# A trunk of two layers on one core: the last token tile's last chunk in two halves, norms of fewer single-column operations, stores on two queues

## The chip, the core and the metric

The kernel runs on one core of a Trainium2 chip. A core has a tensor engine (PE, with its weight loads shown as PEld), a vector engine (DVE), a scalar engine (ACT), GpSimd (POOL) and a sync engine (SP) that here only issues transfers; 16 DMA engines move data between the chip's memory and the core. Each engine works through its own instructions in order, and they wait for one another by semaphores. The metric is device time in microseconds, the median of several executions.

## The reference, cut to what matters

256 tokens of 2048 features pass two layers. Layer 0 mixes with a long convolution and a short gated one, layer 1 with centred moving means; after each comes a squared-ReLU MLP with 8192 hidden features. Every part has a norm before and behind it:

```python
def rmsnorm(u, g):
    r = lax.rsqrt(jnp.mean(u * u, axis=-1, keepdims=True) + NORM_EPS)
    return u * r * g

for i in range(2):
    h = rmsnorm(x, g[0])
    m = mixer of layer i (h)
    x = x + rmsnorm(m, g[1])
    h = rmsnorm(x, g[2])
    f = square(relu(h @ mlp_w1[i])) @ mlp_w2[i]
    x = x + rmsnorm(f, g[3])
return x
```

## The kernel before

The tokens are two tiles of 128 (t = 0 and 1). Where tokens lie on the partitions, `xt` [128, 2, 2048] holds x and `ac` [128, 2, 2048] the sum of a projection, in four chunks of 512 features. All weights stream from memory once, in pieces of [128, 1024], by SP's queue into four buffers (`raw`). For precision each operand of a matmul is split into a high and a low part: for weights ACT copies the high part (`whi`, L131) and DVE subtracts it for the low part (`wlo`, L145), and each product is made of three matmuls, high by high, high by low, low by high. The order of work on every engine is written out by hand: instructions are issued in the order in which the Python code runs, and each engine keeps that order.

The MLP's second projection runs in four groups g of 2048 hidden features and four chunks n of 512 columns. A chunk has 8 pieces, and `a_piece` (L251) makes the six matmuls of 512 columns of one piece and one token tile (L258, L259, L260), so a chunk is 48 matmuls a tile. `after_2` (L813) adds the result, scaled by a number for each token, to `ac` (L819), and for the last group `sums` (L667) squares it on ACT with a running sum into a column of `st` (L668), and DVE multiplies the gain of the norm in (L822). `st` is a small tile of single columns.

`rsqrt_of` (L338) makes one over the root mean square of a tile's tokens: a sum over the four parts (L342), a root on ACT (L343), the mean on DVE (L344), then what a `filler` brings, then a reciprocal (L347) and one step of refinement (L348, L349, L350), each on one column. `m_rms` uses it for `ac`, `x_rms` for x; `residual` (L690) then adds a chunk of `ac` times that column to `xt`.

Between two phases stands `boundary` (L745): the last chunk of a phase and the first of the next run token tile by token tile, so that the matmuls of one tile cover the norm, the residuals and the transposes (`x_to_features`, L698) of the other. `unit_pass` (L714) runs one tile over the pieces and issues such steps at given pieces. Layer 1 has two such changeovers: from layer 0's MLP to the pooling (around 1110 to 1145 us), where `m_rms` of tile 1 and `x_rms` of tile 0 stand close together, and from the pooling to the MLP (1155 to 1185 us), where `m_rms` of tile 0 has the gain of the last pooling group as its filler (L931) and PE has nothing to do until `xt` is there. `turn_first` (L799) turns the MLP's first hidden features.

The end is written in three lines: the last chunk for tile 0, then `finish(0)`, the last chunk for tile 1, then `finish(1)`. `finish` (L984) calls `m_rms`, and for each of four chunks `residual` and a store of [128, 512] on SP's queue (L988).

Of the kernel before, what the change touches and what calls it, by code (L numbers as in the profile page):

```python
# [29 lines left out]
# Column tiles of the input projection: x0 0-7, x1 8-15, v 16-23, gb 24-31, gc 32-39, xv 40-47.  # L30
# [13 lines left out]
# Column tiles after which the convolution's parts are issued. For each quarter of the channels and each half:  # L44
# the filter's last layer, and from the quarter's first column tile on, u to tokens, forward and inverse transform.
# [4 lines left out]
# The column tile after which 1 / rms is made.  # L50
R_AT = 2

# Offsets of the per-channel parameters in their array.
# [5 lines left out]
class Stream:  # L59
    """Pieces of [128, 1024] in the order of their use: loaded ahead, split ahead, then used."""  # L60
# [28 lines left out]
    def raw(self, ap, fn, place=None):  # L89
        """fn gets the piece in its turn; place() gives a tile for it that isn't one of the ring's."""  # L90
        self.items.append(("r", ap, (fn, place)))
# [22 lines left out]
    def hi(self, upto):  # L114
        """The high part of the next piece, if a slot is free."""
        if self.n_split >= self.n_dma:
            return False
        i = self.n_split
        kind, ap, what = self.items[i]
        if kind == "w":  # L120
            if what > upto:
                return False
            pool, tag, bufs = self.rings[self.ring_at % len(self.rings)]
            old = self.history[tag]
            if len(old) >= bufs and old[-bufs] >= self.released:
                return False
            old.append(what)
            self.ring_at += 1
            hi = pool.tile([P, 1024], F32R, tag=tag + "h", name="whi", bufs=bufs)
            lo = pool.tile([P, 1024], F32R, tag=tag + "l", name="wlo", bufs=bufs)  # L130
            self.nc.scalar.copy(hi, self.raws[i])  # L131
            self.half.append((i, what, hi, lo))
        elif kind == "r":
            what[0](self.own.pop(i) if what[1] else self.raws.pop(i))
        elif kind == "s":
            what()
        self.n_split += 1
        return True

    def lo(self):  # L140
        """The low part of the oldest piece that has only its high part."""
        if not self.half:
            return False
        i, what, hi, lo = self.half.pop(0)
        self.nc.vector.tensor_tensor(lo, self.raws.pop(i), hi.bitcast(F32), ALU.subtract)  # L145
        self.parts[what] = (hi, lo)
        return True
# [8 lines left out]
    def pump(self, at):  # L156
        """Issue what may run ahead of piece `at`."""
        while True:
            moved = self.load()
            if not self.held or at not in self.parts:  # L160
                upto = at if self.held else at + self.ahead
                moved = self.hi(upto) or moved
                while self.half and (not self.held or self.half[0][1] <= at):
                    moved = self.lo()
            if not moved:
                return
# [13 lines left out]
def trunk(ctx: ExitStack, tc: tile.TileContext, x, xT_d, win_d, wout_d, w1s_d, w1_d, w2_d, pw_d,  # L180
# [23 lines left out]
    st = common.tile([P, 48], F32, name="st")  # L204
    A.dma_start(out=par, in_=par_d)
    make_identity(nc, ident)
    V.memset(eps, EPS)
    A.copy(st[:, 46:47], eps)

    # ---- the stream of pieces  # L210
# [8 lines left out]
    def split_to(hi, lo, src, scale=None):  # L219
        """hi + lo = src * scale, each of 12 bits."""  # L220
        if scale is None:
            A.copy(hi, src)  # L222
            V.tensor_tensor(lo, src, hi.bitcast(F32), ALU.subtract)  # L223
        else:
            A.activation(hi, src, AF.Copy, scale=scale)
            V.scalar_tensor_tensor(lo, src, scale, hi.bitcast(F32), ALU.mult, ALU.subtract)
# [5 lines left out]
    # ---- matmuls  # L232
    def b_tile(pieces, width):
        """[128 features, tokens] of one tile of 128 features."""
# [16 lines left out]
    def a_piece(acc, t, src, k0, part, first, last):  # L251
        """Adds two k-tiles of 512 features to acc [128 tokens of tile t, 512]."""
        hi, lo = part
        for kk in range(2):
            sh = src(k0 + kk)[:, t * P:(t + 1) * P]
            sl = src(k0 + kk)[:, 256 + t * P:256 + (t + 1) * P]
            a, b = hi[:, kk * 512:(kk + 1) * 512], lo[:, kk * 512:(kk + 1) * 512]
            mm(acc, sh, a, start=first and kk == 0, stop=False)  # L258
            mm(acc, sh, b, start=False, stop=False)  # L259
            mm(acc, sl, a, start=False, stop=last and kk == 1)  # L260
# [11 lines left out]
    # ---- mixer of layer 0  # L272
# [44 lines left out]
    def add_squares(q):  # L317
        """The sum of x * x over the k-tiles of a piece, added to that of the pieces before."""
# [18 lines left out]
    # st: 0-7 sums of squares by part; 8.. work by tile  # L337
    def rsqrt_of(parts, t, filler=()):  # L338
        """st[:, 8 + 4 t] = 1 / sqrt(mean + eps)."""
        w = st[:, 16 + 8 * t:24 + 8 * t]  # L340
        r = st[:, 8 + 4 * t:9 + 4 * t]
        V.tensor_reduce(w[:, 0:1], parts, axis=AX.X, op=ALU.add)  # L342
        A.activation(w[:, 1:2], w[:, 0:1], AF.Sqrt, bias=eps, scale=1.0 / D)  # L343
        V.tensor_scalar(w[:, 2:3], w[:, 0:1], 1.0 / D, EPS, ALU.mult, ALU.add)  # L344
        for f in filler:
            f()
        V.reciprocal(w[:, 3:4], w[:, 1:2])  # L347
        V.scalar_tensor_tensor(w[:, 4:5], w[:, 3:4], w[:, 3:4], w[:, 2:3], ALU.mult, ALU.mult)  # L348
        V.tensor_scalar(w[:, 5:6], w[:, 4:5], -0.5, 1.5, ALU.mult, ALU.add)  # L349
        V.tensor_tensor(r, w[:, 3:4], w[:, 5:6], ALU.mult)  # L350
        return r

# [62 lines left out]
    # -- pieces of the filter  # L415
    def filter_layer(acc, bias, dst):
        """dst = sin(freq * (acc + bias))"""
# [25 lines left out]
    def filter_3(q, l):  # L443
        """Sum and difference of the two filters for 256 channels, split."""
# [18 lines left out]
    def filter_4(q):  # L463
        """The filters' transform: cosine part, sine part, cosine part, by the even and the odd frequencies."""
# [19 lines left out]
    # -- the convolution  # L484
    us, Us, Pq, x0s = {}, {}, {}, {}

    def to_tokens(c):
        """u of 128 channels, as its even and odd halves about the middle, to [tokens, channels], split."""
# [53 lines left out]
    # -- what follows each tile of the input projection  # L542
# [57 lines left out]
    def spread_r():  # L600
        """1 / rms of each token, on every partition."""
# [53 lines left out]
    def spread(row, n):  # L655
        """512 columns of a row, on every partition."""
# [17 lines left out]
    def m_rms(t, *filler):  # L674
        return rsqrt_of(st[:, 4 * t:4 * t + 4], t, steps(*filler))
# [4 lines left out]
    def inv_square(t):  # L680
        """st[:, 40 + t] = 1 / (mean + eps)"""
# [6 lines left out]
    def residual(t, n):  # L688
        """x += ac / rms"""
# [24 lines left out]
    def unit_pass(units, t, src, post, slots, release):  # L714
        """The products of one token tile with the pieces of a chunk; slots: what to issue before a unit."""
# [17 lines left out]
    def steps(*fs):  # L733
        """Closures of (function, arguments...)."""
        return [lambda f=f: f[0](*f[1:]) for f in fs]
# [9 lines left out]
    def boundary(units, src, post, uslots, switch, units2, src2, post2, vslots, wslots):  # L745
        """The last chunk of a phase and the first of the next: tile 1 of the one runs while tile 0's norms and
        transposes are made, tile 0 of the other while tile 1's are."""
# [10 lines left out]
    # ---- output projection of layer 0  # L758
# [8 lines left out]
    ysrc = lambda k: YT[:, k]  # noqa: E731  # L767
    xsrc = lambda k: xT[:, k]  # noqa: E731
# [4 lines left out]
    class Mlp:  # L773
# [52 lines left out]
        def run(self):  # L826
            """All but the first chunk and the last, which is returned with its source."""
            for g in range(4):
# [16 lines left out]
                fsrc = lambda k, fts=fts: fts[k // 4][:, k % 4]  # noqa: E731  # L845
# [17 lines left out]
    class Later:  # L863
        """Stands for what `switch` makes."""
# [25 lines left out]
    # ---- layer 1: pooling  # L890
# [24 lines left out]
    def pool_sums(t, g):  # L915
        """The moving sums less the counts' share: [128 tokens, 512] of tile t."""
# [67 lines left out]
    def finish(t):  # L984
        m_rms(t)
        for n in range(4):
            residual(t, n)
            nc.sync.dma_start(out=out[t][:, ch(n)], in_=xt[:, t, ch(n)])  # L988

    unit_pass(units, 0, fsrc, m1.post_last, {"end": steps((finish, 0))}, False)  # L990
    unit_pass(units, 1, fsrc, m1.post_last, {"end": steps((finish, 1))}, True)
# [4 lines left out]
def _constants():  # L996
# [5 lines left out]
    # The even positions, then the odd ones.  # L1002
# [4 lines left out]
    # [quarter][lag][tile of lags][the same 256 channels twice]  # L1007
# [8 lines left out]
    def table(first, second):  # L1016
        """Two [256, 256] tables, [tile of rows][first hi, lo, second hi, lo][256] for each row of a tile."""
# [3 lines left out]
    # The frequencies (2 f + 1) / 1024 of a turn: the even f, then 255 less each of them.  # L1021
    n = np.arange(256, dtype=np.float64)
    f = (2.0 * np.concatenate([n[0::2], 255.0 - n[0::2]]) + 1.0) * math.pi / 512.0
    # [lag / 2][even or odd lag][cosine, sine][hi, lo][even f]
# [6 lines left out]
    # [token < 128][even or odd f][plus or minus][hi, lo][f]  # L1031
# [17 lines left out]
def _arrange(x, norm_g, mix_w_in, hy_short_w, hy_short_b, hy_filt_w1, hy_filt_b1, hy_filt_w2, hy_filt_b2,  # L1049
# [3 lines left out]
    chan = lambda v: v.reshape(-1, P).T  # noqa: E731  # L1053

    def features(w):
        """[D, n] -> tiles of 128 columns: [tile][row in k-tile][k-tile, column]"""
        return c(w.reshape(KT, P, -1, P).transpose(2, 1, 0, 3)).reshape(-1, P, KT * P)

    def tokens(w, kt):
        """[kt * 128, n] -> chunks of 512 columns: [chunk][row in k-tile][k-tile, column]"""  # L1060
# [48 lines left out]
```

## Time and profile before

| | us |
|---|---|
| runs | 1895.4, 1896.15, 1896.45 (median 1896.15) |
| profiled execution, from its first to its last instruction (span) | 1894.5 |
| PE busy | 1866.0 (98%) |
| DVE busy | 1212.3 (64%) |
| ACT busy | 860.5 (45%) |
| last matmul starts | 1884.72 |
| first and last residual of tile 1 start | 1888.71, 1890.70 |

The profiled execution has no time of its own beside its span; what the runs' clock takes in around the span shows in the runs alone. Matmuls are pipelined: a row's length is longer than the step from one matmul to the next, so steps are read from starts. A row of the timeline gives the start, the length, the engine, the line of the program, the operation, the tiles written and read, the shape, and in brackets how long the engine had been idle and what ended that.

### The profile page before, as it was taken

To read this page: it belongs to the slowest core of one execution; us is meant where nothing else is said; L and a number is where in the kernel's file an instruction comes from. 1 tells how busy PE (TensorE), PEld (TensorE's weight loads), DVE (VectorE), ACT (ScalarE), POOL (GpSimd) and SP (SyncE) were. 2 spreads that over 40 slices of the span, in tenths; PEclk is the share of its full clock that TensorE was granted. 3 is DMA by queue.
4 is the path that set the end of the run, shared out by engine and by line. 5 is a ranking of instruction groups with operands and counts; after the bars stand their busy time and mean duration, and the time that the engine had idled before them with its cause. 6 is when DMAs were issued, how large, how long until landed. Compare 5 with 4: busy or idle time off the path is not lost.

```text
span 1894.5 us, 26333 instructions
## 1 busy us (share of the span) xinstructions
PE 1866.0 (98%) x10278; PEld 1616.6 (85%) x10278; DVE 1212.3 (64%) x1671; ACT 860.5 (45%) x1194; POOL 18.0 (1%) x38
## 2 busy tenths in 40 slices
PE   8999999999999999999999998999999999999998
PEld 7999999888888888888888876888888888888886
DVE  8898997667645654665466569674565456546654
ACT  6433333556444443443344456654444344434441
POOL 0000000000000000000000000000000000000000
PEclk9999999999999999999999999999999999999999
DMA  7655555847666666666666654676666666666662
GB/s 250 223 195 179 183 158 185 281 146 229 202 188 188 191 189 189 190 189 190 188 190 188 199 151 145 197 225 189 187 191 189 189 189 189 190 188 190 188 188 79
DMA packets 99109, 358.71 MB, mean 189 GB/s; under 512 B 11472, under 2 KB 11634, under 8 KB 98728
## 3 DMA queue, kind: packets, MB, share of 16 engines
q1 hardware_dynamic: 95840, 346.73, 58.8%
q0 software_dynamic: 2752, 10.14, 1.8%
q8 instruction: 81, 1.33, 0.3%
q14 instruction: 44, 0.36, 0.1%
q10 hardware_dynamic: 392, 0.16, 0.0%
HBM read 354.88 MB, written 2.10 MB: 188 GB/s over the span
## 4 chain that ended last, share of the span: by engine, by line
PE 94%; DVE 2%; DMA 2%; ACT 1%; issue 0%; DVEq 0%; SPq 0%; ACTq 0%
PE mm L243 23%; PE mm L247 16%; PE mm L259 15%; PE mm L260 15%; PE mm L258 15%; PE mm L245 4%; PE mm L246 4%; DVE wlo L145 1%; DMA raw<-in_w 1%; PE tr L536 1%; DMA raw<-in_win 1%; DMA x<-in_xT 0%; PE tr L451 0%; DVE xt L690 0%; ACT whi L131 0%
## 5 line engine op out<-in xcount | busy, mean ns | idle before, releaser
L145 DVE TENSOR_TENSOR wlo<-raw,whi 128x1024 fp32r<-128x1024 f32 x648 | 787.0, 1224 | 540.4 <-ACT whi L131 535.9
L131 ACT CAST whi<-raw 128x1024 fp32r<-128x1024 f32 x648 | 674.8, 1048 | 671.5 <-PE mm L260 370.1
L247 PE MATMUL mm<-xT,wlo 128*128 128x256 f32 x2688 | 757.5, 282 | 1.0 <-DVE wlo L145 0.9
L243 PE MATMUL mm<-xT,whi 128*128 128x512 f32 x1920 | 666.4, 390 | 0.0
L247 PEld LDWEIGHTS mm<-xT,wlo 128*128 128x128 f32 x2688 | 508.4, 189 | 2.0 <-DVE wlo L145 1.7
L243 PEld LDWEIGHTS mm<-xT,whi 128*128 128x128 f32 x1920 | 360.4, 188 | 75.7
L258 PE MATMUL mm<-whi,ft 128*128 128x512 f32 x1024 | 404.2, 395 | 0.0
L260 PE MATMUL mm<-whi,ft 128*128 128x512 f32 x1024 | 404.0, 395 | 0.0
L259 PE MATMUL mm<-wlo,ft 128*128 128x512 f32 x1024 | 404.0, 395 | 0.0
L260 PEld LDWEIGHTS mm<-whi,ft 128*128 128x128 f32 x1024 | 192.9, 188 | 45.1
L258 PEld LDWEIGHTS mm<-whi,ft 128*128 128x128 f32 x1024 | 192.9, 188 | 44.9
L259 PEld LDWEIGHTS mm<-wlo,ft 128*128 128x128 f32 x1024 | 192.9, 188 | 44.6
L245 PE MATMUL mm<-xT,whi 128*128 128x256 f32 x768 | 217.9, 284 | 8.4 <-ACT whi L131 8.4
L246 PE MATMUL mm<-xT,whi 128*128 128x256 f32 x768 | 215.5, 281 | 0.0
L245 PEld LDWEIGHTS mm<-xT,whi 128*128 128x128 f32 x768 | 145.7, 190 | 9.4 <-ACT whi L131 8.4
L246 PEld LDWEIGHTS mm<-xT,whi 128*128 128x128 f32 x768 | 145.7, 190 | 0.2
L222 ACT CAST ft<-f 128x256 fp32r<-128x256 f32 x120 | 48.8, 407 | 213.0 <-DVE f L810 213.0
L223 DVE TENSOR_TENSOR ft<-f,ft 128x256 fp32r<-128x256 f32 x120 | 51.1, 426 | 56.7 <-ACT ft L222 56.7
L810 DVE SCALAR_TENSOR_TENSOR f<-z 128x256 f32<-128x256 f32 x120 | 50.9, 425 | 4.1
L258 PE MATMUL mm<-whi,YT 128*128 128x512 f32 x128 | 50.8, 397 | 0.0
L260 PE MATMUL mm<-whi,YT 128*128 128x512 f32 x128 | 50.5, 395 | 0.0
L259 PE MATMUL mm<-wlo,YT 128*128 128x512 f32 x128 | 50.5, 394 | 0.0
(174 smaller groups left out, 947.6 us busy)
## 6 DMA issues: line engine op xcount, KB each, us to landing
raw<-in_w SPq DMA_DIRECT2D x496, 512.0 KB, 4.3
raw<-in_win SPq DMA_DIRECT2D x96, 512.0 KB, 4.6
raw<-in_wout SPq DMA_DIRECT2D x32, 512.0 KB, 4.7
raw<-in_w1s SPq DMA_DIRECT2D x16, 512.0 KB, 4.4
g<-in_gb POOLq DMA_DIRECT2D x16, 256.0 KB, 4.1
raw<-in_pw SPq DMA_DIRECT2D x8, 512.0 KB, 4.5
x<-in_xT SPq DMA_DIRECT2D x4, 512.0 KB, 4.8
xt<-in_x POOLq DMA_DIRECT2D x2, 1024.0 KB, 7.2
```

The costliest lines, as they stand in the source:

```text
L131: self.nc.scalar.copy(hi, self.raws[i])
L145: self.nc.vector.tensor_tensor(lo, self.raws.pop(i), hi.bitcast(F32), ALU.subtract)
L222: A.copy(hi, src)
L223: V.tensor_tensor(lo, src, hi.bitcast(F32), ALU.subtract)
L243: mm(acc, a, xT[:, k, :], start=k == 0, stop=False)
L245: mm(acc[:, :256], a, xT[:, k, 0:256], start=k == 0, stop=False)
L246: mm(acc[:, :256], a, xT[:, k, 256:512], start=False, stop=False)
L247: mm(acc[:, :256], b, xT[:, k, 0:256], start=False, stop=k == 15)
L258: mm(acc, sh, a, start=first and kk == 0, stop=False)
L259: mm(acc, sh, b, start=False, stop=False)
L260: mm(acc, sl, a, start=False, stop=last and kk == 1)
L810: V.scalar_tensor_tensor(f, z, 0.0, z, ALU.max, ALU.mult)
```

## The change

1. Tile 1's last chunk is made in two halves of 256 columns, one after the other over all 8 pieces (`half_chunk`): 96 matmuls of 256 columns in place of 48 of 512. The first half's scale, square and gain are issued ahead of the second half.
2. The sum of squares known before the last part is reduced and scaled ahead (`known_of`), and the last part enters the root as its input with the known part as its bias. So in `finish` the sum over parts is gone from behind the last square, and for tile 1 the last half's gain is the filler.
3. `rsqrt_of` works with half of the reciprocal root: four times the mean in, and the refinement in two operations instead of three (L348, L352, L353, L354 in the new numbering). This holds for all ten norms made on token tiles. The epsilon comes from a tile (`eps4`).
4. `finish` makes five residuals, three of 512 columns and two of 256, and stores each on SP's and ACT's queue in turn.

Comments are removed as well, and `st` has one column more.

```diff
-    def rsqrt_of(parts, t, filler=()):
-        """st[:, 8 + 4 t] = 1 / sqrt(mean + eps)."""
+    def rsqrt_of(parts, t, filler=(), known=None):
         w = st[:, 16 + 8 * t:24 + 8 * t]
         r = st[:, 8 + 4 * t:9 + 4 * t]
-        V.tensor_reduce(w[:, 0:1], parts, axis=AX.X, op=ALU.add)
-        A.activation(w[:, 1:2], w[:, 0:1], AF.Sqrt, bias=eps, scale=1.0 / D)
-        V.tensor_scalar(w[:, 2:3], w[:, 0:1], 1.0 / D, EPS, ALU.mult, ALU.add)
+        if known is None:
+            V.tensor_reduce(w[:, 0:1], parts, axis=AX.X, op=ALU.add)
+            parts, known = w[:, 0:1], eps4
+        A.activation(w[:, 1:2], parts, AF.Sqrt, bias=known, scale=4.0 / D)
+        V.tensor_scalar(w[:, 2:3], parts, -4.0 / D, known, ALU.mult, ALU.subtract)
         for f in filler:
             f()
         V.reciprocal(w[:, 3:4], w[:, 1:2])
         V.scalar_tensor_tensor(w[:, 4:5], w[:, 3:4], w[:, 3:4], w[:, 2:3], ALU.mult, ALU.mult)
-        V.tensor_scalar(w[:, 5:6], w[:, 4:5], -0.5, 1.5, ALU.mult, ALU.add)
-        V.tensor_tensor(r, w[:, 3:4], w[:, 5:6], ALU.mult)
+        V.scalar_tensor_tensor(r, w[:, 4:5], 3.0, w[:, 3:4], ALU.add, ALU.mult)
         return r
+
+    def known_of(parts, t):
+        w = st[:, 16 + 8 * t:24 + 8 * t]
+        V.tensor_reduce(w[:, 6:7], parts, axis=AX.X, op=ALU.add)
+        V.tensor_scalar(w[:, 7:8], w[:, 6:7], 4.0 / D, 4.0 * EPS, ALU.mult, ALU.add)
+        return w[:, 7:8]
...
-    def finish(t):
-        m_rms(t)
-        for n in range(4):
-            residual(t, n)
-            nc.sync.dma_start(out=out[t][:, ch(n)], in_=xt[:, t, ch(n)])
-
-    unit_pass(units, 0, fsrc, m1.post_last, {"end": steps((finish, 0))}, False)
-    unit_pass(units, 1, fsrc, m1.post_last, {"end": steps((finish, 1))}, True)
+    def finish(t, known, last, *filler):
+        rsqrt_of(last, t, filler, known)
+        r = st[:, 8 + 4 * t:9 + 4 * t]
+        cuts = [slice(c, c + 512) for c in (0, 512, 1024)] + [slice(1536, 1792), slice(1792, 2048)]
+        for i, at in enumerate(cuts):
+            V.scalar_tensor_tensor(xt[:, t, at], ac[:, t, at], r, xt[:, t, at], ALU.mult, ALU.add)
+            (nc.sync, nc.scalar)[i % 2].dma_start(out=out[t][:, at], in_=xt[:, t, at])
+
+    def half_chunk(t, h, part):
+        acc = bank()[:, 0:256]
+        for u, (n, k0, _, first_, last_) in enumerate(units):
+            S.pump(n)
+            hi_, lo_ = S.get(n)
+            for kk in range(2):
+                sh = fsrc(k0 + kk)[:, t * P:(t + 1) * P]
+                sl = fsrc(k0 + kk)[:, 256 + t * P:256 + (t + 1) * P]
+                at = slice(kk * 512 + h * 256, kk * 512 + h * 256 + 256)
+                mm(acc, sh, hi_[:, at], start=first_ and kk == 0, stop=False)
+                mm(acc, sh, lo_[:, at], start=False, stop=False)
+                mm(acc, sl, hi_[:, at], start=False, stop=last_ and kk == 1)
+        o = ac[:, t, 1536 + 256 * h:1792 + 256 * h]
+        V.scalar_tensor_tensor(o, acc, st[:, 40 + t:41 + t], o, ALU.mult, ALU.add)
+        A.activation(junk()[:, 0:256], o, AF.Square, accum_out=st[:, part:part + 1])
+        return lambda: V.tensor_tensor(o, o, m1.g3[3][:, h * 256:(h + 1) * 256], ALU.mult)
+
+    known = known_of(st[:, 0:3], 0)
+    unit_pass(units, 0, fsrc, m1.post_last, {"end": steps((finish, 0, known, st[:, 3:4]))}, False)
+    half_chunk(1, 0, 7)()
+    known = known_of(st[:, 4:8], 1)
+    gain = half_chunk(1, 1, 48)
+    finish(1, known, st[:, 48:49], gain)
+    for n, *_ in units:
+        S.done(n)
```

How the instructions stand. DVE's end of the program, from tile 1's last scale on, before:

```order
L819 SCALAR_TENSOR_TENSOR ac<-mm,st,ac 128x512
L822 TENSOR_TENSOR ac<-ac,g 128x512
L342 TENSOR_REDUCE st<-st 128x1
L344 TENSOR_SCALAR st<-st 128x1
L347 RECIPROCAL st<-st 128x1
L348 SCALAR_TENSOR_TENSOR st<-st 128x1
L349 TENSOR_SCALAR st<-st 128x1
L350 TENSOR_TENSOR st<-st 128x1
L690 SCALAR_TENSOR_TENSOR xt<-ac,st,xt 128x512 x4
```

and now, from the first half's scale on (L1017 scale, L1019 gain, L359 and L360 the known part, L1000 the residuals):

```order
L1017 SCALAR_TENSOR_TENSOR ac<-mm,st,ac 128x256
L1019 TENSOR_TENSOR ac<-ac,g 128x256
L359 TENSOR_REDUCE st<-st 128x1
L360 TENSOR_SCALAR st<-st 128x1
L1017 SCALAR_TENSOR_TENSOR ac<-mm,st,ac 128x256
L348 TENSOR_SCALAR st<-st 128x1
L1019 TENSOR_TENSOR ac<-ac,g 128x256
L352 RECIPROCAL st<-st 128x1
L353 SCALAR_TENSOR_TENSOR st<-st 128x1
L354 SCALAR_TENSOR_TENSOR st<-st 128x1
L1000 SCALAR_TENSOR_TENSOR xt<-ac,st,xt 128x512 x3
L1000 SCALAR_TENSOR_TENSOR xt<-ac,st,xt 128x256 x2
```

The gain has moved in between the one operation that needs the last square (L348) and the reciprocal (L352), the sum is gone from there, and one small operation before the residuals.

ACT's end of the program, before (L668 squares, L343 root):

```order
L131 CAST whi<-raw 128x1024 x7
L668 ACTIVATE junk,st<-ac 128x512 x3
L343 ACTIVATE st<-st,eps 128x1
L668 ACTIVATE junk,st<-ac 128x512
L343 ACTIVATE st<-st,eps 128x1
```

and now (L678 and L1018 squares, L347 root, L1001 stores):

```order
L131 CAST whi<-raw 128x1024 x7
L678 ACTIVATE junk,st<-ac 128x512 x3
L347 ACTIVATE st<-st 128x1
L1001 DMA out<-xt 128x512
L1001 DMA out<-xt 128x256
L1018 ACTIVATE junk,st<-ac 128x256 x2
L347 ACTIVATE st<-st 128x1
L1001 DMA out<-xt 128x512
L1001 DMA out<-xt 128x256
```

Two store issues of each tile stand in ACT's order now, tile 0's ahead of the squares of tile 1's halves.

DVE at layer 1's second changeover, from the sums of the last pooling group on, before (L342 to L350 are tile 0's norm, L931 the gain, L690 the residuals):

```order
L926 SCALAR_TENSOR_TENSOR ac<-mm,par,psb 128x512 x2
L342 TENSOR_REDUCE st<-st 128x1
L344 TENSOR_SCALAR st<-st 128x1
L931 TENSOR_TENSOR ac<-ac,g 128x512
L347 RECIPROCAL st<-st 128x1
L348 SCALAR_TENSOR_TENSOR st<-st 128x1
L349 TENSOR_SCALAR st<-st 128x1
L350 TENSOR_TENSOR st<-st 128x1
L690 SCALAR_TENSOR_TENSOR xt<-ac,st,xt 128x512 x2
```

and now (L345 to L354 the norm, `eps_83` the new epsilon's tile, L941 the gain, L700 the residuals):

```order
L936 SCALAR_TENSOR_TENSOR ac<-mm,par,psb 128x512 x2
L345 TENSOR_REDUCE st<-st 128x1
L348 TENSOR_SCALAR st<-st,eps_83 128x1
L941 TENSOR_TENSOR ac<-ac,g 128x512
L352 RECIPROCAL st<-st 128x1
L353 SCALAR_TENSOR_TENSOR st<-st 128x1
L354 SCALAR_TENSOR_TENSOR st<-st 128x1
L700 SCALAR_TENSOR_TENSOR xt<-ac,st,xt 128x512 x2
```

One operation is gone between the reciprocal and the residuals; nothing else has moved.

More of the change, by code (lines that the diff above doesn't have):

```diff
@@ L203, in trunk @@
     eps = common.tile([P, 1], F32, name="eps")
-    st = common.tile([P, 48], F32, name="st")
+    st = common.tile([P, 49], F32, name="st")
     A.dma_start(out=par, in_=par_d)
@@ L207, in trunk @@
     V.memset(eps, EPS)
+    eps4 = common.tile([P, 1], F32, name="eps4")
+    V.memset(eps4, 4.0 * EPS)
     A.copy(st[:, 46:47], eps)
```

## The prediction

> **What bounds the kernel now.** I read the page's chain first, then the timeline of the last ten microseconds engine by engine, then the places where the tensor engine (PE) waits.
>
> The page's fourth part, shares of the span on the chain that ended last:
> ```profile
> PE 94%; DVE 2%; DMA 2%; ACT 1%; issue 0%; DVEq 0%; SPq 0%; ACTq 0%
> ```
> PE carries the run, so a change counts only where PE waits or after its last matmul. Those are two kinds of place, and the diff touches both.
>
> First the end. The vector engine's (DVE) timeline of the tail: start, length, line, tiles.
> ```profile
> 1885.16 0.75 DVE L819 SCALAR_TENSOR_TENSOR ac<-mm,st,ac 128x512 f32<-128x512 f32 x1 [4.85 <-PE mm L260]
> 1886.76 0.69 DVE L822 TENSOR_TENSOR ac<-ac,g 128x512 f32<-128x512 f32 x1 [0.85 <-ACT junk L668]
> 1887.37 0.15 DVE L342 TENSOR_REDUCE st<-st 128x1 f32<-128x4 f32 x1
> 1887.55 0.15 DVE L344 TENSOR_SCALAR st<-st 128x1 f32<-128x1 f32 x1
> 1887.88 0.16 DVE L347 RECIPROCAL st<-st 128x1 f32<-128x1 f32 x1 [0.17 <-ACT st L343]
> 1888.08 0.22 DVE L348 SCALAR_TENSOR_TENSOR st<-st 128x1 f32<-128x1 f32 x1
> 1888.33 0.15 DVE L349 TENSOR_SCALAR st<-st 128x1 f32<-128x1 f32 x1
> 1888.52 0.16 DVE L350 TENSOR_TENSOR st<-st 128x1 f32<-128x1 f32 x1
> 1888.71 2.74 DVE L690 SCALAR_TENSOR_TENSOR xt<-ac,st,xt 128x512 f32<-128x512 f32 x4
> ```
> and the scalar engine's (ACT) at the same place:
> ```profile
> 1886.00 0.63 ACT L668 ACTIVATE junk<-ac 128x512 f32<-128x512 f32 x1 [9.31 <-DVE ac L819]
> 1886.54 0.19 ACT L668 ACTIVATION_READ_ACCUMULATOR junk<-ac 128x1 f32 x1
> 1887.55 0.29 ACT L343 ACTIVATE st<-st,eps 128x1 f32<-128x1 f32 x1 [0.83 <-DVE st L342]
> ```
> No other work hides this: scale (L819), square (L668), gain (L822), sum, root, five small operations, four residuals. The first residual ends at 1888.71 + 0.75 = 1889.46. Then the stores, by windows (PE, PEld, DVE, ACT, POOL busy; granted clock, DMA share, GB/s), with the issue row of the last four (KB each, us to landing):
> ```profile
> 1890.33:1893.08 2.75, 0.00 (x0) 0.00 (x0) 1.12 (x2) 0.00 (x0) 0.00 (x0) 0.50 1.00 378
> 1893.08:1894.50 1.42, 0.00 (x0) 0.00 (x0) 0.00 (x0) 0.00 (x0) 0.00 (x0) 0.50 0.01 3
> ```
> ```profile
> out<-xt SPq DMA_DIRECT2D x4, 256.0 KB, 2.1
> ```
> The 16 DMA engines are full from 1890.33 to 1893.08, 1 MB at 378 GB/s. So the end hangs on when the first residual is ready, not on the last: 1893.08 is 3.62 us after 1889.46, and the last 1.42 us are landing and the closing barrier.
>
> Second, PE's waits in the middle, from its timeline:
> ```profile
> 1132.92 0.49 PE L259 MATMUL mm<-wlo,xT 128*128 128x512 f32 x1 [2.20 <-DVE wlo L145]
> 1164.55 0.66 PE L698 MATMUL tr<-ident,xt 128*128 128x128 f32 x4 [3.64 <-DVE xt L690]
> 1177.52 0.50 PE L259 MATMUL mm<-wlo,xT 128*128 128x512 f32 x1 [0.58 <-DVE wlo L145]
> ```
> All three stand in layer 1's two changeovers, each behind DVE work with a norm in it.
>
> **The change, part by part: PE.** The last 48 matmuls of 512 columns become 96 of 256. First and last row of the 48 in the tail, then 37 successive matmuls of 256 columns in the input projection, each with its own weight load, as the new ones have:
> ```profile
> 1873.81 0.39 PE L258 MATMUL mm<-whi,ft 128*128 128x512 f32 x1
> ...
> 1884.72 0.40 PE L260 MATMUL mm<-whi,ft 128*128 128x512 f32 x1
> ```
> ```profile
> 299.76 0.28 PE L246 MATMUL mm<-xT,whi 128*128 128x256 f32 x1
> ...
> 303.96 0.28 PE L246 MATMUL mm<-xT,whi 128*128 128x256 f32 x1
> ```
> Before: the last starts 10.91 us after the first and ends 0.40 later, 11.31. After: 4.20 / 36 = 0.1167 a step, 95 steps 11.08, plus 0.28: 11.36. **+0.05.** The first half's post-work (some 2 us on DVE and ACT) lies beside the second half's 5.6 us of matmuls.
>
> **The tail's chain.** Widths of 256 and 1024 from the groups by form (busy, mean ns):
> ```profile
> L555 DVE SCALAR_TENSOR_TENSOR x<-zp,par,x 128x256 f32<-128x256 f32 x16 | 7.7, 484 | 0.6
> ```
> ```profile
> L810 DVE SCALAR_TENSOR_TENSOR f<-z 128x256 f32<-128x256 f32 x120 | 50.9, 425 | 4.1
> ```
> ```profile
> L223 DVE TENSOR_TENSOR ft<-f,ft 128x256 fp32r<-128x256 f32 x120 | 51.1, 426 | 56.7 <-ACT ft L222 56.7
> ```
> ```profile
> L321 ACT ACTIVATE x<-x 128x1024 f32<-128x1024 f32 x4 | 4.0, 1051 | 0.0
> ```
> 1. Scale: 0.75 to 0.48 (L555's form, a scalar read from a tile): −0.27.
> 2. Square: 1024 columns take 1.05, 512 take 0.63, so 256 some 0.42: −0.21.
> 3. From the accumulator (1886.54 + 0.19 = 1886.73) to the reciprocal (1887.88) pass 1.15 us: gain, sum, root in a row. Now the root starts straight from the accumulator, done after 0.03 + 0.29 = 0.32. DVE meanwhile does one small operation and the half gain. That pair stands already in layer 1 with 512 columns:
> ```profile
> 1162.24 0.15 DVE L344 TENSOR_SCALAR st<-st 128x1 f32<-128x1 f32 x1
> 1162.32 0.68 DVE L931 TENSOR_TENSOR ac<-ac,g 128x512 f32<-128x512 f32 x1
> 1162.91 0.15 DVE L347 RECIPROCAL st<-st 128x1 f32<-128x1 f32 x1
> ```
> The small one holds up the gain by 0.08; its new scalar operand adds 0.06 (L555 less L810). The gain holds up the reciprocal by 0.59, 0.09 less than its length; at 256 (L223) 0.43 − 0.09 = 0.34. Sum 0.03 + 0.14 + 0.34 = 0.51, so DVE and not the root ends last: −0.64.
> 4. Reciprocal to first residual: 0.83 now (1887.88 to 1888.71). L349 and L350, 0.19 each from start to start, become one operation with a constant. No row shows that form at one column. At 0.22 like L348 it would take 0.25 to the next start, saving 0.13; 0.06 shorter, as L810 is against L555, 0.19. I take −0.19, since it has L810's operands.
>
> Sum −1.31; bounds −1.2 and −1.4, with up to 0.06 for simpler waits before the square.
>
> **Stores.** Five per tile instead of four, the last two of 128 KB in rows of 1 KB, alternating between SP and ACT. With the engines full, a smaller last store starts no earlier. Its shorter rows cost something that no row shows; I take **+0.05**, bounds 0 and +0.1. On the gain side: if only the last store's own way counted, 128 KB at 378 GB/s less, −0.3. The full window speaks for the first. [...]
>
> ACT gains four store issues, each waiting for a residual. For tile 0, ACT's queue then holds the first half's square, which needs DVE behind the same residuals anyway; all of it ends some 3 us before PE does. The tile's two single-column operations for the known part of the sum lie there too.
>
> Tail: 0.05 − 1.31 + 0.05 = −1.21.
>
> **The changeovers.** Each norm loses 0.19 between reciprocal and what follows; the new operand's 0.06 before it costs only where the root doesn't hide it. At 1128–1138 two norms stand in a row in the chain (start, length):
> ```profile
> 1131.57 0.16 DVE st L350
> 1131.73 1.14 DVE wlo L145
> ```
> so PE's wait that ended at 1132.92 shrinks by 2 × 0.19 = 0.38; what follows shifts as a whole. Before 1164.55 there is one norm with the gain beside it: −0.19 + 0.06 = −0.13. Before 1177.52 another: −0.19. Sum **−0.70**. With the dearer form −0.46. The other four norms of the changeovers stand where PE doesn't wait: nothing. What is late next is the weight stream, from the waits at 1189–1206 (us in total, times, longest):
> ```profile
> ACT whi L131 <- DMA raw<-in_w: 7.6, 6, 2.3
> ```
> Its loads are issued as DVE frees buffers, so they should move earlier with DVE; if not, the gain is swallowed, down to 0. I keep −0.70, for the chain names those norms.
>
> **Sum.** −1.21 − 0.70 = −1.91 on a span of 1894.5. The median of the runs, 1896.15, lies 1.65 above; taking that as fixed: **1894.2 us**, 0.10% less. A measurement of this kernel can tell about 0.2% (3.8 us) from no change, so this counts as no change.
>
> **Rivals.**
> *The middle gives nothing* (the weight stream, above): only the tail, 1896.15 − 1.21 = 1894.9. For it: 7.6 us of waits on loads. Against: most loads there are issued after DVE's own steps.
>
> *More than I count.* The last store's 0.3 comes after all: 1893.9. Or the clock: after the 3.64 us wait the granted clock (the third number from the end) falls, and the matmuls spread,
> ```profile
> 1166.00:1167.00 1.00, 1.00 (x4) 0.68 (x4) 0.82 (x4) 0.42 (x2) 0.00 (x0) 0.50 0.00 0
> ```
> ```profile
> 1168.51 0.77 PE L698 MATMUL tr<-ident,xt 128*128 128x128 f32 x4
> ```
> ```profile
> 1167.51 1.41 DVE L690 SCALAR_TENSOR_TENSOR xt<-ac,st,xt 128x512 f32<-128x512 f32 x2
> ```
> and a shorter wait could avert that. It is worth little: at full clock these transposes could start when the first of the two residuals is written, 0.75 after 1167.51, or 1168.26, so 0.25 us sooner: 1893.9. Behind them DVE rules until 1177.52. [...]
>
> *Slower: the store on ACT's queue.* The trace has stores on SP's queue alone. What ACT issued, at the start:
> ```profile
> par<-in_par ACTq DMA_DIRECT2D x1, 96.0 KB, 5.0
> ```
> The fourth store, the last on ACT, is ready 2.5 steps of 0.66 (L690's row: 2.74 less 0.75, by three) after the first residual, 1.7 us. Today's last store lands 3 × 0.66 + 2.1 = 4.1 after it, 4.15 with the shorter rows. At 5.0 the fourth lands at 6.7, 2.5 late: 1894.2 + 2.5 = 1896.7. From a landing of 4.4 us on the change's gain is gone. [...]
>
> *Much slower: weight loads come into the open.* A load's own length is, from the page's groups,
> ```profile
> L247 PEld LDWEIGHTS mm<-xT,wlo 128*128 128x128 f32 x2688 | 508.4, 189 | 2.0 <-DVE wlo L145 1.7
> ```
> If the 96 came at 0.189 instead of 0.1167, 6.9 us more: 1901.1. Break-even is 0.1167 + 1.91 / 96 = 0.137. Against it: the 37 rows above have just such loads and step at 0.1167.
>
> *The change doesn't do what it says:* the order of instructions shows the halves, the shorter norms and both queues in place, so I give this no chance of its own.
>
> **How the numbers follow.** Chances: the forecast 0.66, its own range 1893.5 to 1894.8 (chain −1.2 to −1.4, stores 0 to 0.1, middle −0.46 to −0.75, and some 0.3 for how runs differ, their spread being 1895.4 to 1896.45); the middle gives nothing 0.14; more than I count 0.12; ACT's queue 0.04; weight loads 0.02; something unseen 0.02. The range 1893.1 to 1895.9 takes in the first three, down to tail, store and clock together (1894.2 − 0.3 − 0.25, with the spread), and up to half the chain's gain. Faster by over 0.2% (under 1892.4) none of the cases reaches: 0.03 for what I don't see. Slower by over 0.2% (above 1899.9) is the weight loads: 0.03. Within: 0.94.
>
> **What would show it.** Right: 96 matmuls at 0.117 a step; from PE's end to the first residual's end about 3.0 us instead of 4.34; the reciprocal waiting on DVE's gain and not on the root; full DMA engines for 2.8 us behind the first store's 0.8; a first wait near 1133 of 1.8 us, the one near 1164 of 3.5, the one near 1177 of 0.4. Wrong: if DMA engines idle between the last stores, or if ACT's stores land later than SP's, the store terms are wrong; if the waits shrink and the tail starts no earlier, the gain went into the weight stream.

## The result and the profile after

| | before | after |
|---|---|---|
| runs beside one another, median (lowest to highest) | 1896.3 us (1895.4 to 1896.5), 4 | 1913.87 us (1912.89 to 1914.36), 4 |
| ratio, 95% interval | | 1.0093 [1.008, 1.0106] |
| span of the profiled execution | 1894.5 | 1911.7 |
| PE busy | 1866.0 | 1884.7 |
| span less PE busy | 28.5 | 27.0 |

The change makes the kernel 17.6 us slower, 0.93%; 1894.2 was forecast. The last two rows of the table say where to look. The time in which PE does nothing fell by 1.5 us, about what the forecast had reckoned with. PE's busy time rose by 18.7. The page's first part after, and the shares of the chain that ended last:

```profile
PE 1884.7 (99%) x10326; PEld 1620.1 (85%) x10326; DVE 1213.2 (63%) x1668; ACT 861.1 (45%) x1196; POOL 18.0 (1%) x38
```
```profile
PE 97%; DVE 1%; DMA 1%; ACT 1%; issue 0%; SPq 0%; DVEq 0%; ACTq 0%
```

PE's share of the chain went from 94% to 97%, and 48 matmuls more (10278 to 10326) can't be 18.7 us. So old matmuls became longer. The page's costliest groups, of before and then of after (count, then busy us and mean ns of one; busy counts overlapping matmuls once, so it is the sum to compare):

```profile
L247 PE MATMUL mm<-xT,wlo 128*128 128x256 f32 x2688 | 757.5, 282 | 1.0 <-DVE wlo L145 0.9
L243 PE MATMUL mm<-xT,whi 128*128 128x512 f32 x1920 | 666.4, 390 | 0.0
...
L258 PE MATMUL mm<-whi,ft 128*128 128x512 f32 x1024 | 404.2, 395 | 0.0
```
```profile
L249 PE MATMUL mm<-xT,wlo 128*128 128x256 f32 x2688 | 757.3, 282 | 1.2 <-DVE wlo L145 1.2
L245 PE MATMUL mm<-xT,whi 128*128 128x512 f32 x1920 | 678.5, 397 | 0.0
...
L260 PE MATMUL mm<-whi,ft 128*128 128x512 f32 x1008 | 398.7, 396 | 0.0
```

The 1920 matmuls of the MLP's first projection (L243, now L245) are the same instructions on tiles of the same shape, and take 12.1 us more. The timeline of PE shows that they do so in steady work, where PE waits for nothing: one group of the first projection, 512 matmuls, first and last, and the chunk group behind it, 384 matmuls, first and last. Before:

```profile
587.61 0.40 PE L243 MATMUL mm<-xT,whi 128*128 128x512 f32 x1
...
676.26 0.28 PE L247 MATMUL mm<-xT,wlo 128*128 128x256 f32 x1
676.37 0.39 PE L258 MATMUL mm<-whi,ft 128*128 128x512 f32 x1
...
765.37 0.40 PE L260 MATMUL mm<-whi,ft 128*128 128x512 f32 x1
```
After:
```profile
592.29 0.40 PE L245 MATMUL mm<-xT,whi 128*128 128x512 f32 x1
...
600.04 0.40 PE L245 MATMUL mm<-xT,whi 128*128 128x512 f32 x1
600.28 0.28 PE L249 MATMUL mm<-xT,wlo 128*128 128x256 f32 x1
600.41 0.39 PE L245 MATMUL mm<-xT,whi 128*128 128x512 f32 x1
600.63 0.28 PE L249 MATMUL mm<-xT,wlo 128*128 128x256 f32 x1
600.75 0.40 PE L245 MATMUL mm<-xT,whi 128*128 128x512 f32 x1
...
682.61 0.28 PE L249 MATMUL mm<-xT,wlo 128*128 128x256 f32 x1
682.72 0.40 PE L260 MATMUL mm<-whi,ft 128*128 128x512 f32 x1
...
772.10 0.39 PE L262 MATMUL mm<-whi,ft 128*128 128x512 f32 x1
```

The first projection's group takes 88.65 us before and 90.32 after, the chunk group 89.00 and 89.38. Within a group one matmul of 512 columns takes 0.24 us to the next start and the other 0.22 to 0.23, in turn; before, each took 0.23. In the whole run the last matmul starts 18.07 us later (1884.72, 1902.79): 2.9 of these have come when the first long run of `a_piece` begins (315.8, 318.7), the eight groups of the first projection bring 12.1, those of `a_piece` with layer 0's changeover 3.5, and layer 1's changeovers give 0.5 back. The delay grows with the work, about 1.7 us in each group of 512 matmuls, and jumps nowhere.

The waits that the forecast spoke of, PE after:

```profile
1143.38 0.50 PE L261 MATMUL mm<-wlo,xT 128*128 128x512 f32 x1 [1.82 <-DVE wlo L145]
1147.31 0.50 PE L261 MATMUL mm<-wlo,xT 128*128 128x512 f32 x1 [1.82 <-DVE wlo L145]
...
1175.02 1.12 PE L708 MATMUL tr<-ident,xt 128*128 128x128 f32 x4 [3.52 <-DVE xt L700]
```

And the tail, on all engines:

```profile
1902.79 0.28 PE L1015 MATMUL mm<-whi,ft 128*128 128x256 f32 x1
1903.11 0.48 DVE L1017 SCALAR_TENSOR_TENSOR ac<-mm,st,ac 128x256 f32<-128x256 f32 x1 [3.81 <-PE mm L1015]
1903.63 0.42 ACT L1018 ACTIVATE junk<-ac 128x256 f32<-128x256 f32 x1 [5.04 <-DVE ac L1017]
1903.95 0.19 ACT L1018 ACTIVATION_READ_ACCUMULATOR junk<-ac 128x1 f32 x1
1904.17 0.21 DVE L348 TENSOR_SCALAR st<-st 128x1 f32<-128x1 f32 x1 [0.58 <-ACT junk L1018]
1904.17 0.29 ACT L347 ACTIVATE st<-st 128x1 f32<-128x1 f32 x1
1904.30 0.42 DVE L1019 TENSOR_TENSOR ac<-ac,g 128x256 f32<-128x256 f32 x1
1904.63 0.16 DVE L352 RECIPROCAL st<-st 128x1 f32<-128x1 f32 x1
1904.82 0.22 DVE L353 SCALAR_TENSOR_TENSOR st<-st 128x1 f32<-128x1 f32 x1
1905.08 0.16 DVE L354 SCALAR_TENSOR_TENSOR st<-st 128x1 f32<-128x1 f32 x1
1905.27 2.87 DVE L1000 SCALAR_TENSOR_TENSOR xt<-ac,st,xt 128x512 f32<-128x512 f32 x5
```

Then the stores, by windows (columns as in the forecast: PE, PEld, DVE, ACT, POOL busy; clock, DMA share, GB/s), and behind them the same two stretches of before, each cut where the last data is through:

```profile
1906.90:1909.90 3.00, 0.00 (x0) 0.00 (x0) 1.24 (x3) 0.00 (x0) 0.00 (x0) 0.67 0.96 346
1909.90:1911.72 1.82, 0.00 (x0) 0.00 (x0) 0.00 (x0) 0.00 (x0) 0.00 (x0) 0.50 0.00 0
```
```profile
1890.33:1893.25 2.92, 0.00 (x0) 0.00 (x0) 1.12 (x2) 0.00 (x0) 0.00 (x0) 0.50 0.95 358
1893.25:1894.53 1.28, 0.00 (x0) 0.00 (x0) 0.00 (x0) 0.00 (x0) 0.00 (x0) 0.50 0.00 0
```

The transfers take 3.00 us instead of 2.92, and from the last data to the end of the span pass 1.82 us instead of 1.28.

### The profile page after: what moved, and what is told of

It is laid out like the page before. It is cut to its first block, busy times and chain, and to the rows that moved or that the text cites. A ratio compares the mean times of both kernels' runs of the same rounds, so it can differ in the third digit from the quotient of the medians.

```text
span 1911.7 us, 26430 instructions
## 1 busy us (share of the span) xinstructions
PE 1884.7 (99%) x10326; PEld 1620.1 (85%) x10326; DVE 1213.2 (63%) x1668; ACT 861.1 (45%) x1196; POOL 18.0 (1%) x38
## 4 chain that ended last, share of the span: by engine, by line
PE 97%; DVE 1%; DMA 1%; ACT 1%; issue 0%; SPq 0%; DVEq 0%; ACTq 0%
PE mm L245 24%; PE mm L249 17%; PE mm L261 15%; PE mm L260 15%; PE mm L262 15%; PE mm L247 5%; PE mm L248 5%; DMA raw<-in_win 1%; PE tr L546 1%; PE tr L461 0%; PE tr L708 0%; PE mm L708 0%; DVE wlo L145 0%; PE mm L932 0%; PE mm L1015 0%; PE mm L1013 0%
## 5 line engine op out<-in xcount | busy, mean ns | idle before, releaser
L245 PE MATMUL mm<-xT,whi 128*128 128x512 f32 x1920 | 678.5, 397 | 0.0
L245 PEld LDWEIGHTS mm<-xT,whi 128*128 128x128 f32 x1920 | 360.5, 188 | 88.9
L260 PE MATMUL mm<-whi,ft 128*128 128x512 f32 x1008 | 398.7, 396 | 0.0
L261 PE MATMUL mm<-wlo,ft 128*128 128x512 f32 x1008 | 398.5, 395 | 0.0
L262 PE MATMUL mm<-whi,ft 128*128 128x512 f32 x1008 | 398.5, 395 | 0.0
L260 PEld LDWEIGHTS mm<-whi,ft 128*128 128x128 f32 x1008 | 189.4, 188 | 45.8
L262 PEld LDWEIGHTS mm<-whi,ft 128*128 128x128 f32 x1008 | 189.4, 188 | 45.8
```

The costliest lines, as they stand in the source:

```text
L245: mm(acc, a, xT[:, k, :], start=k == 0, stop=False)
```

## The experiments

All kernels of this part but three (e2, e8, e9) are the kernel before with unused bytes put between its tiles, so that no instruction changes. Addresses are bytes within each partition of the core's memory (SBUF), where the built programs put the tiles. Before: `xT` (the input of the first projection) at 16512, `st` at 50592, the landing buffers `raw` from 50784, the weights' ring `whi` and `wlo` from 67168 (five buffers each) and again from 154208 (five each), `ft` (the hidden features, the other operand of the chunks) from 196576. The buffers stand multiples of 256 bytes apart, so counted modulo 256 every weight buffer lies at 96, `xT` at 128 and `ft` at 224. In the changed kernel the 49th column of `st` costs 32 bytes more and `eps4` another 32 (`eps`, 4 bytes of data, takes 32 in the built program too), so `raw`, the weights, `xt` and `ac` stand 64 bytes further, while `xT`, in front of them, and `ft`, which is placed from the other end, stay.

The theory was *placement*: these 64 bytes alone make PE slower. The rivals: the instructions that changed; loads or copies, whose buffers moved too; and, within placement, the place of the weights by itself against their distance from the operand that PE reads with them.

**e1: 64 bytes and nothing else.**

```diff
     st = common.tile([P, 48], F32, name="st")
+    common.tile([P, 16], F32, name="pad")
```

> The kernel before with an unused tile of 64 bytes behind st: every tile allocated after it (weights, xt, ac) moves by 64 bytes, as in the changed kernel; no instruction differs. Theory P (placement): the changed kernel is slower because the two parts of each weight piece lie 64 bytes further on, so PE's steps of 512 columns alternate between 229 and 240 ns: about 1913 us (1911 to 1915). Theory I (instructions): the slower steps come from the changed instructions themselves; without them 1896.3 us, as before.

Measured: 1915.31 us (1913.71 to 1916.44) against 1895.56, ratio 1.0103 [1.0089, 1.0117]. From the page's groups:

```profile
L244 PE MATMUL mm<-xT,whi 128*128 128x512 f32 x1920 | 678.5, 397 | 0.0
...
L259 PE MATMUL mm<-whi,ft 128*128 128x512 f32 x1024 | 405.2, 396 | 0.0
```

The first projection's 678.5 us is that of the changed kernel to the tenth. An unused tile of 64 bytes costs what the whole change costs.

**e2: the change without the 64 bytes.** `eps` becomes a tile of 8 columns, which still takes 32 bytes; `eps4` is its second column and the 49th sum its third.

```diff
-    eps = common.tile([P, 1], F32, name="eps")
-    st = common.tile([P, 49], F32, name="st")
+    eps_ = common.tile([P, 8], F32, name="eps")
+    eps, eps4 = eps_[:, 0:1], eps_[:, 1:2]
+    st = common.tile([P, 48], F32, name="st")
...
-    eps4 = common.tile([P, 1], F32, name="eps4")
...
-    gain = half_chunk(1, 1, 48)
-    finish(1, known, st[:, 48:49], gain)
+    gain = half_chunk(1, 1, eps_[:, 2:3])
+    finish(1, known, eps_[:, 2:3], gain)
```

> The changed kernel with all its instructions, but the new single columns put into the spare room of the eps tile, so that every other tile lies where it lay before. Theory P: the steps are those of before, and what is left is the prediction's own sum, 1894.2 us (1893.5 to 1894.8). Theory I: about 1913 us.

Measured: 1894.57 us (1893.15 to 1896.17) against 1895.56, ratio 0.9993 [0.9984, 1.0002]. Page:

```profile
PE 1866.2 (99%) x10326; PEld 1619.2 (86%) x10326; DVE 1212.1 (64%) x1668; ACT 860.6 (45%) x1196; POOL 18.0 (1%) x38
...
L245 PE MATMUL mm<-xT,whi 128*128 128x512 f32 x1920 | 666.4, 390 | 0.0
```

Every instruction of the change is there, PE's busy time is back (1866.0 before) and so is the kernel's time. The span is 1892.8, 1.7 less than before; the gain that the medians show, 1.0, isn't clear of noise, for the interval takes in 1.

**e3 and e4: 32 and 128 bytes**, the same line as in e1 with 8 and 32 columns.

> The kernel before moved by 32 bytes: the weights start on a multiple of 64 bytes. Theory P gives no number of its own for this: between 1896 and 1914 us, by how the step depends on the place; PE's steps of 512 columns tell. Theory I: 1896.3 us.

> The kernel before moved by 128 bytes. Theory P: if the steps depend on the place within 128 bytes, 1896.3 us as before; if on a longer period, another time. Theory I: 1896.3 us.

Measured: e3 1914.74 us (1914.35 to 1920.46), ratio 1.0108 [1.0094, 1.0121]; e4 1877.17 us (1876.78 to 1879.01), ratio 0.9904 [0.9891, 0.9918]. The groups of e4:

```profile
L244 PE MATMUL mm<-xT,whi 128*128 128x512 f32 x1920 | 666.3, 392 | 0.0
...
L259 PE MATMUL mm<-whi,ft 128*128 128x512 f32 x1024 | 398.6, 389 | 0.0
```

So the place before wasn't the best one. With 128 bytes the chunks are quicker than ever (398.6 for 404.2 us on this line, and as much on two more), the first projection is as before, and an unused tile makes the kernel 18 us faster.

**e5: the weights at the place of e1, and `xT` moved with them.** The 64 bytes stand ahead of `xT`.

```diff
+    common.tile([P, 16], F32, name="pad")
     xT = common.tile([P, KT, 512], F32R, name="xT")
```

> The kernel before with 64 unused bytes ahead of xT, so that xT moves with the weights and their distance stays that of before; only the tiles on the far side of the memory (YT and the hidden features ft) stay, and so their distance to the weights changes as in e1. Theory D (distance: PE reads a weight piece and the activations at a time, and the step is set by how far apart the two lie): the pairs of the MLP's first projection (xT with weights, 512 and 256 columns) take 347 ns as before, where e1 has 354; the chunks of its second projection (ft with weights) stay as in e1; together about 1901 us. Theory A (the place of the weights alone): 1914 to 1915 us as e1.

Measured: 1898.31 us (1897.09 to 1900.62) against 1895.57, ratio 1.0014 [1.0003, 1.0024]:

```profile
L244 PE MATMUL mm<-xT,whi 128*128 128x512 f32 x1920 | 666.2, 390 | 0.0
...
L259 PE MATMUL mm<-whi,ft 128*128 128x512 f32 x1024 | 405.2, 396 | 0.0
```

This is the run that separates the two forms of the theory. The weights have e1's addresses. The first projection, whose other operand moved along, has its old 666 us; the chunks, whose other operand `ft` stayed, keep e1's 405.2: 1.0 us more than before on each of three lines, and the kernel is 2.7 us slower, less than the 5 expected. So the place of the weights alone doesn't set the step: it matters where the other operand of the matmul stands. This is shown for the first projection, at one pair of places; no run moved `ft` with the weights.

**e6 and e7: which of the moved tiles.** e6 has the 64 bytes between `raw` and the weights, so the loads' landing buffers stay; e7 has them behind the first ring of weight buffers, so half the weight buffers stay. The line takes the 64 bytes from a pool of its own and stands at those places.

```diff
+    ctx.enter_context(tc.tile_pool(name="gap", bufs=1)).tile([P, 16], F32, name="pad")
```

> The 64 unused bytes stand behind the four buffers into which the weights are loaded, so these stay and the split parts move. Theories D and A: as e1, 1914 to 1915 us. Theory R (the loads or their reading by the scalar and vector engines are what is disturbed): 1895.6 us as before.

> The 64 unused bytes stand behind the first five buffers of the split parts; the second five, which come into use after the input projection, move, and xt and ac with them. Theories D and A: matmuls with the first five keep 228 ns for 512 columns, those with the second five alternate around 234, so about half of e1's loss: 1903 to 1906 us. If it is xt, ac or anything else that moves and not the weights: 1914 or 1895.6 us, and no difference between the two fives.

Measured: e6 1913.49 us (1913.15 to 1913.83), ratio 1.0095 [1.0075, 1.0116]; e7 1903.06 us (1902.96 to 1904.96), ratio 1.0043 [1.0027, 1.0059]. The first projection in e6, then in e7:

```profile
L244 PE MATMUL mm<-xT,whi 128*128 128x512 f32 x1920 | 678.5, 397 | 0.0
```
```profile
L244 PE MATMUL mm<-xT,whi 128*128 128x512 f32 x1920 | 672.4, 394 | 0.0
```

The loads' buffers have no part in it, and half the weight buffers cost half: 672.4 is the middle of 666.4 and 678.5.

**e8: the change, at the better place.** e2 with the 128 bytes of e4 behind `st`.

```diff
     st = common.tile([P, 48], F32, name="st")
+    common.tile([P, 32], F32, name="pad")
```

> The changed kernel at home (e2) moved by 128 bytes as in e4. If the gain of the place (18.4 us in e4) and that of the instructions (1.0 us in e2, 1.9 by the prediction) add up: 1875.3 to 1876.2 us, faster than the kernel before by 1.0%.

Measured: 1877.12 us (1876.57 to 1878.35) against 1895.57, ratio 0.9906 [0.9889, 0.9922]:

```profile
PE 1847.9 (99%) x10326; PEld 1613.6 (86%) x10326; DVE 1212.1 (65%) x1668; ACT 862.2 (46%) x1196; POOL 18.0 (1%) x38
```

This version is 0.9% faster than the kernel before and about 1.9% faster than the changed one (1913.87). Nearly all of the 0.9% is the place: e4, without the change, has 1877.17. The expected 1875.3 to 1876.2 is missed; what the change adds isn't resolved in these medians.

**e9: all stores of the end on SP's queue**, in e2's kernel.

```diff
-            (nc.sync, nc.scalar)[i % 2].dma_start(out=out[t][:, at], in_=xt[:, t, at])
+            nc.sync.dma_start(out=out[t][:, at], in_=xt[:, t, at])
```

> The changed kernel with every buffer at its old place (as e2), and all stores of the end on SP's queue again. Theory: the prediction's store term (+0.05) was too small because stores that alternate between two queues land later: then from the first residual's end to the span's end some 5.1 us pass, as before the change, in place of 5.7, and the span is about 0.5 us shorter than e2's. Rival: the shorter rows of 1 KB cost it, or the earlier start of the first store beside unchanged landings: then 5.6 to 5.7 remain with SP alone. One look; the medians cannot tell half a microsecond, so the rows of the tail decide.

Measured: one run, 1894.31 us, span 1892.5. Its first residual ends at 1886.84, so 5.69 us pass to the end of the span; in the changed kernel 5.70 (1906.02 to 1911.72), before 5.07. By windows, and SP's waits:

```profile
1887.72:1890.70 2.98, 0.00 (x0) 0.00 (x0) 1.23 (x3) 0.00 (x0) 0.00 (x0) 0.50 0.94 349
1890.70:1892.53 1.83, 0.00 (x0) 0.00 (x0) 0.00 (x0) 0.00 (x0) 0.00 (x0) 0.50 0.00 0
```
```profile
SPq L1142 <- DMA out<-xt: 1.6, 2, 1.2
```

The theory falls, as far as one profile of each goes: alternating the queues doesn't cost the half microsecond, nor does it gain anything. What both have, and the kernel before has not, is five stores, the last two of 128 KB in rows of 1 KB. Whether the one or the other makes the half microsecond wasn't tried.

**e10, e11, e12: 192, 256 and 512 bytes.**

> Before, with 192 unused bytes behind the small tile st. If the steps depend on the distance between the two operands with a period of 256 bytes, 192 is the mirror of 64: slower, 1910 to 1918. If a further 128 bytes always gains what it gained from 0 to 128: 1896 to 1898. If places were irrelevant: 1896.

> The same with 256 unused bytes. Period of 256 bytes: the old steps of 228 and 118 ns and 1895 to 1897. A longer period (512 or more): another time, which side is open.

> The same with 512 unused bytes. Period of 256 or 512 bytes: 1895 to 1897 with the old steps. If neither e11 nor this run returns to them, no short period holds and a place has to be measured each time.

Measured against 1895.87: e10 1897.29 us (1896.02 to 1898.96), ratio 1.0007 [0.9995, 1.0018]; e11 1894.79 (1894.64 to 1895.99), 0.9996 [0.9984, 1.0007]; e12 1894.98 (1894.49 to 1896.98), 0.9999 [0.9988, 1.001]. The groups of e10 and of e11:

```profile
L244 PE MATMUL mm<-xT,whi 128*128 128x512 f32 x1920 | 672.8, 393 | 0.0
...
L259 PE MATMUL mm<-whi,ft 128*128 128x512 f32 x1024 | 398.6, 389 | 0.0
```
```profile
L244 PE MATMUL mm<-xT,whi 128*128 128x512 f32 x1920 | 666.4, 390 | 0.0
...
L259 PE MATMUL mm<-whi,ft 128*128 128x512 f32 x1024 | 404.1, 395 | 0.0
```

At 256 and at 512 bytes everything is as before. e10 has the time of before by another sum: a slower first projection and quicker chunks. The mirror of 64 that I had expected at 192 bytes isn't there.

Put together (us from the first to the last start in a group of 512 matmuls of the first projection and of 384 in the chunks, layer 0's second group; the distance of the weights from the other operand modulo 256):

| bytes | weights − `xT` | first projection | weights − `ft` | chunks | kernel |
|---|---|---|---|---|---|
| 0 (before) | 224 | 88.65 | 128 | 89.0 | 1895.6 to 1896.3 |
| 32 (e3) | 0 | 90.3 | 160 | 89.7 | 1914.74 |
| 64 (e1) | 32 | 90.3 | 192 | 89.4 | 1915.31 |
| 128 (e4) | 96 | 88.6 | 0 | 86.8 | 1877.17 |
| 192 (e10) | 160 | 89.5 | 64 | 87.7 | 1897.29 |
| 256 (e11) | 224 | 88.7 | 128 | 89.0 | 1894.79 |
| 64, with `xT` (e5) | 224 | 88.6 | 192 | 89.4 | 1898.31 |

## Why the prediction was wrong, point by point

**The step that failed** is the first conclusion: "PE carries the run, so a change counts only where PE waits or after its last matmul." It holds as long as every matmul keeps its step, and that was assumed without a term. The sum has +0.05 for PE, for the 48 matmuls that became 96, and nothing for the other ten thousand. The two lines that moved the tiles, the 49th column of `st` and the tile `eps4`, were seen in the change and costed at nothing. PE's busy time is 1884.7 us with them and 1866.2 in e2, which has the change without them, so they cost 18.5 us; e1 has the loss without the change.

None of the rivals held it. The rival by which weight loads come into the open was about PE's step and came nearest in size, 1901.1, but it put the loss into the 96 new matmuls. Those run at (1902.79 − 1891.60) / 95 = 0.118 us a step, where 0.117 was forecast; from the first one's start to the last one's end this is 11.47 us, 0.16 more than the 48 took before, where 0.05 was forecast.

**What the sum did say is tested by e2**, which has the change and the old addresses: 1894.57 against the forecast of 1894.2. Beside the kernel before this is 1.0 us less, where 1.91 was summed, and the interval takes in both no change and the whole sum. The span of the profiled executions is 1.7 shorter, but not all of that is the change's, as the end of this part shows. Term by term:

- *The tail's chain*, forecast −1.31: from PE's end to the first residual's end 4.34 before, 1903.07 to 1906.02 = 2.95 after, so −1.39. The scale took 0.48 and the square 0.42, as taken from the rows of other widths. From the accumulator (1904.14) to the reciprocal (1904.63) pass 0.49 where 0.51 was worked out; the root ends at 1904.46 and the gain at 1904.72, so the reciprocal follows the gain, as said. From there to the first residual 0.64 instead of 0.83, the −0.19 forecast. What is left, 0.08, is for the most part the shorter wait before the square (0.09 before, 0.04 after), which the bounds allowed for.
- *The stores*, forecast +0.05, measured +0.63 (5.07 to 5.70). The transfers themselves came out about as said: 3.00 us instead of 2.92, +0.08. No row of before showed what rows of 1 KB cost, and the +0.05 was a choice between bounds; after, the full engines moved 340 GB/s with them (1909.0 to 1909.6) and 394 with the rows of 2 KB ahead of them (1908.0 to 1908.8). The rest, +0.54, is what follows them: when the last data is through, at 1909.90, another 1.82 us pass, where before 1893.25 to 1894.53 were 1.28; SP's wait for the stores takes this up (1.8 us in two waits, 1.3 before). The forecast had no term for this closing stretch and so left it as it was. The rival of a late store on ACT's queue is not the cause, as e9 shows with SP alone, and in the changed kernel ACT's stores landed 2.2 to 2.3 us after their issue (medians), as SP's did, where the rival had 5.0.
- *The changeovers*, forecast −0.70: the first wait was to be 1.8 and is 1.82, the one near 1164 was to be 3.5 and is 3.52. Other profiles agree: 1.84 and 3.52 in e2, and with the instructions of before 2.21 and 3.66 in e11. The third, near 1177, was to be 0.4, but it comes and goes without the change: 0.58 before, 0.16 in e11, none in e12. The whole stretch that holds layer 1's changeovers, from the first matmul of layer 0's last group of chunks to layer 1's first projection, takes 173.83 us before (1032.36 to 1206.19), 174.09 in e11 and 172.83 in e12; it takes 173.44 in e2 and 172.73 in e9. So with the same instructions it differs by more than 0.70, and the sum of this term is neither confirmed nor refuted. One thing that differs between executions is PE's pace behind the first wait: matmuls of 512 columns step there by 0.43 us in e2 (1132.33 to 1133.61), as the changed kernel's do at a granted clock of 0.50 (1177.22 to 1178.93), and by 0.23 before (1133.25 to 1133.95), where 1.00 was granted. Behind the wait near 1164 a clock of 0.50 was granted in both kernels, after 3.64 us (1166 to 1168) and after 3.52 (1175 to 1178): the shorter wait did not avert it.

So the tail gave −1.39 + 0.63 = −0.76 where −1.26 was forecast for these two. In e2 the last matmul ends 0.99 us sooner than before (1885.12, 1884.13), and most of this is not the change's. PE's first long run of `a_piece` begins, before and then in e2, at

```profile
315.82 0.39 PE L258 MATMUL mm<-whi,YT 128*128 128x512 f32 x1
```
```profile
314.99 0.39 PE L260 MATMUL mm<-whi,YT 128*128 128x512 f32 x1
```

so 0.83 us are there already, ahead of every norm and every matmul that the change touches; e11 and e12, without the change, begin at 315.23 and 315.31. The changeovers bring 0.39 (173.83 less 173.44), and the last chunk takes 0.23 more with its halves. With the tail's 0.76 that makes the 1.7 of the span, of which 0.9 falls into changed work, near the 1.0 of the medians and half of the 1.91 forecast. That 1894.57 lies so near to 1894.2 is in part luck: the kernel before was itself quicker in that comparison, 1895.56 where the forecast started from 1896.15.

## What to carry to other kernels

Where PE carries the run, read the sizes and the order of the tiles in a diff as part of the change: compare the addresses that the build gives, and if the matmuls' operands have moved against one another, count every matmul as changed. Split a surprise on the page into PE's busy time and the rest of the span before looking for waits: here 18.7 us stood in the one and −1.5 in the other. And try a few paddings of 32 to 192 bytes between the operands; in this kernel the best of them is worth 18 us or 1%, where the change's instructions bring about 1 us in e2, and it changes no work.

## What the runs showed of the hardware that I had not expected

In this kernel the step of a matmul in a steady stream depends on where its two operands stand to one another in SBUF (e1 and e5, for the first projection). A pair of 512 and 256 columns of the first projection takes (88.65 + 0.12) / 256 = 0.347 us before and (90.32 + 0.12) / 256 = 0.353 with the weights 64 bytes further (the 0.12 is the last matmul's own step); a chunk's matmul takes 89.0 / 383 = 0.232 us before and 86.8 / 383 = 0.227 at 128 bytes. At 256 and 512 bytes the times are those of before (88.7 and 89.0 us for the two groups in e11, the kernel 1894.79 there and 1894.98 in e12); at 128 they are not (86.8 for the chunks and 1877.17 in e4). Between the same instructions at other addresses the kernel's time differs by 2% (1915.31 us in e1, 1877.17 in e4). It isn't the clock, which was granted at 1.00 from 600 to 640 us, in the midst of such a group, before, in the changed kernel, in e1 and in e4; and it isn't where the loads land (e6, 1913.49 us with the landing buffers in their old place).

What inside the chip makes it so was not measured: no run here looked at the read of one operand without that of the other. Nor is the distance all of it: at 32 bytes (e3) the groups of the first projection take 90.3 us in layer 0 and 88.6 in layer 1, at the same addresses. And no simple rule says which distance is good: 0 is the best that the chunks were given, and one of the worst for layer 0's first projection.
